# Experts of a three-layer network: PSUM tiles dealt out anew, and the second group's rows located earlier

## The chip, the cores and the metric

The kernel runs on one core of one Trainium2 chip. The metric is the device time of one execution in microseconds (us). Three executions of the kernel before took 1882.86, 1884.65 and 1886.02 us; the median, 1884.65 us, is the time that a prediction is set against.

## The reference, cut to what matters

The network has three layers over 512 tokens of width 1024: two of mixers and dense feed-forward blocks, and one of attention followed by a mixture of experts. The change lies in that mixture alone, the last part of the program:

```python
def _hierarchical_moe(xt, w_rg, b_rg, w_re, b_re, w_gate, w_up, w_down):
    ...
    expert_id = g_idx * EXPERTS_PER_GROUP + top_i
    combine = jnp.sum(jax.nn.one_hot(expert_id, N_EXPERTS, dtype=jnp.float32)
                      * (g1 * g2)[..., None], axis=1).astype(xt.dtype)
    y = jnp.zeros_like(xt)
    for e in range(N_EXPERTS):
        he = jax.nn.silu(xt @ w_gate[e]) * (xt @ w_up[e])
        y = y + combine[:, e:e + 1] * (he @ w_down[e])
    return y
```

There are 32 experts; every token goes to two of them. Each expert has a gate and an up matrix of 1024 x 256 and a down matrix of 256 x 1024, 3 MB of float32 in all. After the sum the tokens are normalized once more and written out.

## The kernel before, in words

Routing (`tail`, L1506) gives every token two experts and a slot among the 64 rows that each expert has room for. The normalized tokens lie in DRAM (`hd`). The function `moe` (L1626) then works on **pairs** of experts (two times 64 rows fill the 128 partitions; 16 pairs, numbered p) and on **groups** of two pairs (8 groups, numbered g). Its steps are small functions:

- `locate(g)` (L1632) finds which token sits in which of the group's 256 slots. Four `pick`s on VectorE (L1486 to L1488, one for each 128 tokens) write the one-hot matrix `s1`; group 0's were made during routing. Eight place products on TensorE (L1641, six columns each, four for each pair) give each slot's token number and gate weight in a PSUM tile; VectorE makes an index (`ix`, L1644), ScalarE copies two columns (`wsl`, L1650), VectorE adds them (`ws`, L1653), and GpSimd starts an indirect gather (L1646) of the pair's 128 rows from `hd` into `xg`, of which there are three buffers.
- `spread(g)` (L1657) transposes `s1` on TensorE (L1662, two PSUM tiles) and ScalarE copies it (`ST`, L1665). `s1` is one buffer: the next group's picks write it after these transposes.
- `turn(p, j)` (L1668) transposes one half of the gathered rows (L1675, four transposes into one PSUM tile), copied to `mhT` by VectorE (j = 0, L1680) or ScalarE (j = 1, L1678).
- `gate_up(p)` (L1682) is 16 matmuls in one PSUM tile (L1688), then SiLU on ScalarE (`msi`, L1691) and the product on VectorE (`mhe`, L1694).
- `inner(p)` (L1698) transposes `mhe` (L1701, one PSUM tile); ScalarE copies it (`heT`, L1703).
- `down(p)` (L1706) is eight matmuls in two PSUM tiles (L1711), taken out by ScalarE (L1716) and VectorE (L1717).
- `combine(g)` (L1721) adds a group's results to the tokens: 32 matmuls in eight PSUM tiles (L1729), each added by VectorE (L1732).

TensorE's order is written out by hand (`manual_schedule`): what stands first in the program runs first there. The order of the other engines is planned by the framework, which also chooses which of a tag's buffers a tile gets. PSUM has eight banks, and every tile here takes one. They are dealt out by tags: `psum(mm=4, tp=2, px=2)` at L1529 gives four to matrix products (`mm`), two to transposes and place products (`tp`) and two to the combination (`px`). A new tile of a tag waits until the readers of the tile that it replaces are done.

The loop's order for each pair p is: `turn(p + 2, 0)`, `inner(p)`, `turn(p + 2, 1)`, `down(p)`, `gate_up(p + 1)`, and then `locate(p // 2 + 2)` after an even p, or `combine(p // 2)` and `spread(p // 2 + 2)` after an odd one.

SyncE's queue issues the weights: the gate and up matrices of a pair (4 MB, `unit`, L1610) go into rings that hold three pairs, the down matrices (2 MB, `load_down`, L1603) into a ring of two. A pair's next load is issued once the matmuls that read the buffer are done: `load_up(3)` behind `gate_up(0)`, `load_down(p + 2)` behind `down(p)`, `load_up(p + 4)` behind `gate_up(p + 1)`. Three pairs of the one and two of the other are loaded ahead, during routing.

Of the kernel before, what the change touches and what calls it, by code (L numbers as in the profile page):

```python
# [91 lines left out]
class Builder:  # L92
# [1533 lines left out]
    def moe(self, st, s1, weights, downs):  # L1626
        nc = self.nc
        mp = self.pool("moe")
        NG, NPAIR = NE // 4, NE // 2
        grp, rows, hTs = {}, {}, {}  # L1630

        def locate(g):  # L1632

            if g:
                for tt in range(NT):
                    self.pick(g, tt, st, s1)
            ws = []
            for i in range(2):
                pw = self.ps("tp")
                for tt in range(NT):  # L1640
                    nc.tensor.matmul(pw[:, 0:6], s1[:, tt, i * P:(i + 1) * P], st["cw"][:, tt, 2 * g + i, :],  # L1641
                                     start=tt == 0, stop=tt == NT - 1)
                ix = self.t(mp, "ix", [P, 1], U32, bufs=4)
                nc.vector.tensor_scalar(ix, pw[:, 4:5], float(T), None, op0=ALU.add)  # L1644
                xg = self.t(mp, "xg", [P, D], bufs=3)
                nc.gpsimd.indirect_dma_start(xg, None, self.hd[:, :], bass.IndirectOffsetOnAxis(ap=ix, axis=0))  # L1646
                rows[2 * g + i] = xg
                w = self.t(mp, "ws", [P, 1], bufs=6)
                wl = self.t(mp, "wsl", [P, 2], bufs=2)
                nc.scalar.activation(wl, pw[:, 2:4], AF.Copy)  # L1650
                for j in range(2):
                    r = slice(64 * j, 64 * j + 64)
                    nc.vector.tensor_tensor(w[r], pw[r, j:j + 1], wl[r, j:j + 1], op=ALU.add)  # L1653
                ws.append(w)
            grp[g] = [ws]

        def spread(g):  # L1657

            for i in range(2):
                p = self.ps("tp")  # L1660
                for tt in range(NT):
                    nc.tensor.transpose(p[:, tt * P:(tt + 1) * P], s1[:, tt, i * P:(i + 1) * P].bitcast(F32),  # L1662
                                        self.ident)
                s = self.t(mp, "ST", [P, T], F32R, bufs=4)
                nc.scalar.activation(s, p, AF.Copy)  # L1665
                grp[g].append(s)

        def turn(p, j):  # L1668

            xg = rows[p]  # L1670
            if j == 0:
                hTs[p] = self.t(mp, "mhT", [P, KD, P], bufs=2)
            tp = self.ps("tp")
            for i in range(4):
                nc.tensor.transpose(tp[:, i * P:(i + 1) * P], xg[:, (4 * j + i) * P:(4 * j + i + 1) * P], self.ident)  # L1675
            pv = tp.rearrange("p (a b) -> p a b", a=4)
            if j:
                nc.scalar.activation(hTs[p][:, 4:8, :], pv, AF.Copy)  # L1678
            else:
                nc.vector.tensor_copy(hTs[p][:, 0:4, :], pv)  # L1680

        def gate_up(p, u):  # L1682
            ws, hT = grp[p // 2][0], hTs[p]
            ps = self.ps()
            for kb in range(KD):
                for e in range(2):
                    r = slice(64 * e, 64 * e + 64)
                    nc.tensor.matmul(ps[r, :].rearrange("p (j n) -> p j n", j=2), hT[:, kb, r], u[kb // 4][e][:, :, kb % 4, :],  # L1688
                                     start=kb == 0, stop=kb == KD - 1)
            s = self.t(mp, "msi", [P, 256])  # L1690
            nc.scalar.activation(s, ps[:, 0:256], AF.Silu)  # L1691
            he = self.t(mp, "mhe", [P, 256], bufs=2)
            v = lambda z: z.rearrange("t (p k) -> t p k", k=2)
            nc.vector.scalar_tensor_tensor(he.rearrange("t (k p) -> t p k", k=2), v(s), ws[p % 2], v(ps[:, 256:512]),  # L1694
                                           op0=ALU.mult, op1=ALU.mult)
            return he

        def inner(p, he):  # L1698
            tp = self.ps("tp")
            for f in range(2):  # L1700
                nc.tensor.transpose(tp[:, f * P:(f + 1) * P], he[:, f * P:(f + 1) * P], self.ident)  # L1701
            heT = self.t(mp, "heT", [P, 256], bufs=2)
            nc.scalar.activation(heT, tp[:, 0:256], AF.Copy)  # L1703
            return heT

        def down(p, heT, rv):  # L1706
            dn = [self.ps() for _ in range(2)]
            for hf in range(2):
                for f in range(2):
                    for e in range(2):  # L1710
                        nc.tensor.matmul(dn[hf][64 * e:64 * e + 64, :], heT[:, f * P + 64 * e:f * P + 64 * e + 64],  # L1711
                                         rv[e][:, f, hf * 512:(hf + 1) * 512], start=f == 0, stop=f == 1)
            ye = []
            for hf in range(2):
                yh, yl = (z[p % 2 * 2 + hf] for z in self.yroom)
                nc.scalar.activation(yh, dn[hf], AF.Copy)  # L1716
                nc.vector.tensor_tensor(yl, dn[hf], yh.bitcast(F32), op=ALU.subtract)  # L1717
                ye.append((yh, yl))
            return ye

        def combine(g, ye, then=None):  # L1721
            ST = grp[g][1:]
            for tt in range(NT):
                for hf in range(2):
                    p = self.ps("px")
                    n = 0
                    for i in range(2):
                        for z in ye[i][hf]:
                            nc.tensor.matmul(p, ST[i][:, tt * P:(tt + 1) * P], z, start=n == 0, stop=n == 3)  # L1729
                            n += 1  # L1730
                    xs = self.x[:, tt, hf * 512:(hf + 1) * 512]
                    nc.vector.tensor_tensor(xs, p, xs, op=ALU.add)  # L1732
                if then and tt:
                    then(tt - 1)
            if then:
                then(NT - 1)

        with self.tc.manual_schedule(engines={mybir.EngineType.PE}):
            locate(0)
            spread(0)  # L1740
            for j in range(2):
                turn(0, j)
            he = gate_up(0, weights[0])
            weights.append(self.load_up(3))
            for j in range(2):
                turn(1, j)
            locate(1)
            spread(1)
            ye, last = [], None
            for p in range(NPAIR):  # L1750
                if p + 2 < NPAIR:
                    turn(p + 2, 0)
                heT = inner(p, he)
                if p + 2 < NPAIR:
                    turn(p + 2, 1)
                ye.append(down(p, heT, downs[p]))
                if p + 2 < NPAIR:
                    downs.append(self.load_down(p + 2))
                if p + 1 < NPAIR:
                    he = gate_up(p + 1, weights[p + 1])  # L1760
                    if p + 4 < NPAIR:
                        weights.append(self.load_up(p + 4))
                else:
                    last = self.final()
                if p % 2 == 0 and p // 2 + 2 < NG:
                    locate(p // 2 + 2)
                if p % 2:
                    combine(p // 2, ye, last)
                    ye = []
                    if p // 2 + 2 < NG:  # L1770
                        spread(p // 2 + 2)
        self.done(mp)
# [248 lines left out]
```

## Time and profile before

| | us |
|---|---|
| median of three runs | 1884.65 |
| the profiled execution, its own time | 1883.5 |
| its span, first to last instruction | 1881.8 |
| TensorE busy over the span | 1786.6 (95%) |
| VectorE busy | 922.6 (49%) |
| ScalarE busy | 626.5 (33%) |
| GpSimd busy | 164.6 (9%) |

All times in the profile are counted from the span's start. TensorE is busy nearly throughout, but a matmul's record includes pipeline time, and its clock may be at half speed, so the share alone does not say what a stage is worth. The experts begin near 1554 us and the last result is written at the end of the span. The mean granted TensorE clock over the span is 0.971 of full speed.

### The profile page before, as it was taken

The numbers are of one execution on the slowest core, as the hardware profiler recorded it, in microseconds if no ns is written. First come the engines' busy times: TensorE is split into PE (matmuls) and PEld (weight loads), VectorE is DVE, ScalarE is ACT, GpSimd is POOL, SyncE is SP. The second block draws the span as 40 slices with busy tenths as digits, with TensorE's granted clock in tenths as the row PEclk, the third lists the DMA queues.
The fourth block names the chain that finished last, engine by engine and source line by source line (L and its number), as shares of the span: only waits on it lengthen the run. The fifth ranks groups of instructions, "written<-read, shape, count | busy, mean of one in ns | idle before, by whom it ended". The sixth has DMA issues, their size and how long they took to land. (4 is left out here: it accounts for less than half of the span.)

```text
span 1881.8 us, 23441 instructions
## 1 busy us (share of the span) xinstructions
PE 1786.6 (95%) x9314; PEld 1367.1 (73%) x9315; DVE 922.6 (49%) x1637; ACT 626.5 (33%) x1152; POOL 164.6 (9%) x312
## 2 busy tenths in 40 slices
PE   8999999999999999999999999998999976999997
PEld 6788888888799876778888888876876763444443
DVE  7654444444645345555444444465455563334334
ACT  6333222222431334554322222245556421111112
POOL 1001000000232110002000000020000121000000
PEclk9999999999999996999999999999999986999999
DMA  6433223222331301043232232242312294999972
GB/s 231 148 134 132 93 90 105 97 90 90 111 125 56 90 25 44 1 144 103 90 112 90 90 111 90 68 140 87 92 46 83 80 339 176 374 369 376 348 305 86
DMA packets 136308, 257.01 MB, mean 137 GB/s; under 512 B 11319, under 2 KB 88023, under 8 KB 131971
## 3 DMA queue, kind: packets, MB, share of 16 engines
q1 hardware_dynamic: 124000, 231.89, 35.5%
q10 hardware_dynamic: 9282, 13.10, 2.1%
q0 software_dynamic: 2912, 10.49, 1.4%
q8 instruction: 75, 1.23, 0.3%
q14 instruction: 39, 0.31, 0.0%
HBM read 247.04 MB, written 11.03 MB: 137 GB/s over the span
## 5 line engine op out<-in xcount | busy, mean ns | idle before, releaser
L173 PE MATMUL mm<-acth,whi 128*128 128x512 f32 (+2 forms) x968 | 368.9, 381 | 0.0
L174 PE MATMUL mm<-actl,whi 128*128 128x512 f32 (+2 forms) x968 | 365.0, 377 | 0.0
L175 PE MATMUL mm<-acth,wlo 128*128 128x512 f32 (+2 forms) x968 | 364.4, 376 | 0.0
L150 DVE TENSOR_TENSOR wlo<-raw,whi 128x2048 fp32r<-128x2048 f32 (+1 forms) x96 | 218.7, 2279 | 247.6 <-ACT whi L149 247.4
L149 ACT ACTIVATE whi<-raw 128x2048 fp32r<-128x2048 f32 (+1 forms) x96 | 182.5, 1901 | 435.0 <-issue 195.2
L173 PEld LDWEIGHTS mm<-acth,whi 128*128 128x128 f32 (+1 forms) x968 | 182.0, 188 | 35.2 <-issue 2.4
L175 PEld LDWEIGHTS mm<-acth,wlo 128*128 128x128 f32 (+1 forms) x968 | 182.0, 188 | 34.5 <-issue 0.2
L174 PEld LDWEIGHTS mm<-actl,whi 128*128 128x128 f32 (+1 forms) x968 | 182.2, 188 | 33.6 <-issue 1.0
L173 PE MATMUL mm<-whi,acth 128*128 128x256 f32 (+2 forms) x480 | 160.2, 335 | 2.1 <-ACT gate L707 1.7
L174 PE MATMUL mm<-wlo,acth 128*128 128x256 f32 (+2 forms) x480 | 158.1, 330 | 0.6 <-DVE wlo L150 0.6
L175 PE MATMUL mm<-whi,actl 128*128 128x256 f32 (+2 forms) x448 | 145.6, 327 | 0.4 <-DVE actl L204 0.3
L173 PE MATMUL px<-whi,hidh 128*128 128x512 f32 x352 | 137.4, 390 | 0.6 <-DVE macc L331 0.6
L175 PE MATMUL px<-whi,hidl 128*128 128x512 f32 x352 | 137.9, 392 | 0.0
L174 PE MATMUL px<-wlo,hidh 128*128 128x512 f32 x352 | 137.4, 390 | 0.0
L331 DVE TENSOR_TENSOR macc<-px,macc 128x512 f32<-128x512 f32 x144 | 97.6, 688 | 75.3 <-PE px L175 75.3
L173 PEld LDWEIGHTS mm<-whi,acth 128*128 128x128 f32 x480 | 91.4, 191 | 10.2 <-ACT gate L707 1.9
L174 PEld LDWEIGHTS mm<-wlo,acth 128*128 128x128 f32 x480 | 91.2, 190 | 8.4 <-DVE wlo L150 1.3
L175 PEld LDWEIGHTS mm<-whi,actl 128*128 128x128 f32 x448 | 85.1, 190 | 7.2 <-DVE actl L204 1.0
L173 PEld LDWEIGHTS px<-whi,hidh 128*128 128x128 f32 x352 | 66.1, 188 | 16.4 <-DVE macc L331 1.5
L311 DVE TENSOR_TENSOR hidf<-mm,silu 128x512 f32<-128x512 f32 x44 | 30.4, 690 | 94.8 <-PE mm L175 94.8
L175 PEld LDWEIGHTS px<-whi,hidl 128*128 128x128 f32 x352 | 66.1, 188 | 14.1 <-DVE hidl L313 0.5
L174 PEld LDWEIGHTS px<-wlo,hidh 128*128 128x128 f32 x352 | 66.1, 188 | 13.2
(427 smaller groups left out, 2683.8 us busy)
## 6 DMA issues: line engine op xcount, KB each, us to landing
raw<-in_ffn_w_gate SPq DMA_DIRECT2D x22, 1024.0 KB, 5.2
raw<-in_ffn_w_up SPq DMA_DIRECT2D x22, 1024.0 KB, 5.3
raw<-in_ffn_w_down SPq DMA_DIRECT2D x22, 1024.0 KB, 4.8
mixd<-in_w_expert_down SPq DMA_DIRECT2D x16, 1024.0 KB, 6.9
down<-in_w_expert_down SPq DMA_DIRECT2D x16, 1024.0 KB, 9.1
raw<-in_od_w_in SPq DMA_DIRECT2D x12, 1024.0 KB, 5.0
raw<-in_w_expert_gate SPq DMA_DIRECT2D x18, 512.0 KB, 8.4
raw<-in_w_expert_up SPq DMA_DIRECT2D x18, 512.0 KB, 8.3
```

The source lines that it names most:

```text
L149: self.nc.scalar.activation(hi[:, :n], raw[:, :n], AF.Copy)
L150: self.nc.vector.tensor_tensor(lo[:, :n], raw[:, :n], hi[:, :n].bitcast(F32), op=ALU.subtract)
L173: mm(out, l[0], r[0], start=first, stop=False)
L174: mm(out, l[0], r[1], start=False, stop=False)
L175: mm(out, l[1], r[0], start=False, stop=last)
L311: nc.vector.tensor_tensor(hf, pu[f], s, op=ALU.mult)
L331: nc.vector.tensor_tensor(m, p, m, op=ALU.add)
```

## The change

The PSUM pool is released and opened anew at the head of `moe`, with three tiles for matrix products, three for transposes and two for the combination. The place products of `locate` take their tiles from the combination's tag. And `locate(1)` moves from behind the second pair's transposes to the place between `spread(0)` and the first pair's.

```diff
@@ -1627,6 +1627,7 @@
         nc = self.nc
         mp = self.pool("moe")
         NG, NPAIR = NE // 4, NE // 2
+        self.psum(mm=3, tp=3, px=2)
         grp, rows, hTs = {}, {}, {}
 
         def locate(g):
@@ -1636,7 +1637,7 @@
                     self.pick(g, tt, st, s1)
             ws = []
             for i in range(2):
-                pw = self.ps("tp")
+                pw = self.ps("px")
                 for tt in range(NT):
                     nc.tensor.matmul(pw[:, 0:6], s1[:, tt, i * P:(i + 1) * P], st["cw"][:, tt, 2 * g + i, :],
                                      start=tt == 0, stop=tt == NT - 1)
@@ -1738,13 +1739,13 @@
         with self.tc.manual_schedule(engines={mybir.EngineType.PE}):
             locate(0)
             spread(0)
+            locate(1)
             for j in range(2):
                 turn(0, j)
             he = gate_up(0, weights[0])
             weights.append(self.load_up(3))
             for j in range(2):
                 turn(1, j)
-            locate(1)
             spread(1)
             ye, last = [], None
             for p in range(NPAIR):
```

## Rows read from the trace of the kernel before

**Rows 1.** The page's 40 slices of the span: DMA busy share, in tenths.

```profile
DMA  6433223222331301043232232242312294999972
```

**Rows 2.** TensorE's waits, 1605 to 1830 us: total us, times, longest.

```profile
PE tp L1675 <- ACT heT L1703: 5.7, 12, 0.5
PE tp L1675 <- ACT wsl L1650: 5.3, 5, 1.1
```

**Rows 3.** Windows: PE, PEld, DVE, ACT, POOL busy, PEclk, DMA share, GB/s.

```profile
1580.00:1584.00 4.00, 0.00 (x0) 0.00 (x0) 1.78 (x6) 0.00 (x0) 0.00 (x0) 0.50 1.02 415
1588.00:1592.00 4.00, 4.00 (x12) 1.56 (x14) 0.51 (x3) 0.60 (x1) 0.00 (x0) 0.50 0.01 5
1668.28:1705.86 37.58, 35.32 (x166) 16.71 (x164) 15.00 (x34) 6.55 (x14) 1.88 (x2) 0.95 0.96 363
```

**Rows 4.** Timeline of the experts' opening: start, us, engine, line, [idle before <- releaser].

```profile
1558.59 1.23 PE L1641 MATMUL tp<-cw,s 128*128 128x6 f32 x5 [2.43 <-POOL cw L1459]
...
1559.44 1.11 POOL L1646 DMA_INDIRECT xg<-hd,ix  x1 [0.91 <-DVE ix L1644]
...
1564.34 1.94 PE L1675 MATMUL tp<-ident,xg 128*128 128x128 f32 x8 [2.01 <-DMA xg<-hd,ix]
...
1564.66 0.48 DVE L1488 SCALAR_TENSOR_TENSOR s<-iota,sl,sa 128x256 fp32r<-128x256 f32 x1
...
1574.62 1.09 PE L1675 MATMUL tp<-ident,xg 128*128 128x128 f32 x8
...
1577.20 0.94 POOL L1646 DMA_INDIRECT xg<-hd,ix  x1 [15.38 <-DVE ix L1644]
...
1585.87 1.08 PE L1675 MATMUL tp<-ident,xg 128*128 128x128 f32 x4 [6.61 <-DMA xg<-hd,ix]
...
1588.90 5.61 PE L1711 MATMUL mm<-mixd,heT 128*64 128x512 f32 x16
```

**Rows 5.** Timeline of two passages from place products to a down projection.

```profile
1601.30 1.05 PE L1641 MATMUL tp<-cw,s 128*128 128x6 f32 x8
...
1605.33 3.65 PE L1711 MATMUL mm<-down,heT 128*64 128x512 f32 x16
...
1637.42 1.05 PE L1641 MATMUL tp<-cw,s 128*128 128x6 f32 x8
...
1638.59 0.65 DVE L1694 SCALAR_TENSOR_TENSOR mhe<-msi,ws,mm 128x256 f32<-128x256 f32 x1
...
1639.54 0.63 PE L1675 MATMUL tp<-ident,xg 128*128 128x128 f32 x4 [1.06 <-ACT wsl L1650]
1640.00 0.38 PE L1701 MATMUL tp<-ident,mhe 128*128 128x128 f32 x2
...
1640.42 0.38 ACT L1703 ACTIVATE heT<-tp 128x256 f32<-128x256 f32 x1 [1.54 <-PE tp L1701]
...
1641.90 4.71 PE L1711 MATMUL mm<-down,heT 128*64 128x512 f32 x16
```

**Rows 6.** Timeline of one passage from spread to a down projection.

```profile
1623.70 1.03 PE L1662 MATMUL tp<-ident,s 128*128 128x128 f32 x8
...
1624.33 1.09 ACT L1665 ACTIVATE ST<-tp 128x512 fp32r<-128x512 f32 x2 [8.03 <-PE tp L1662]
...
1624.98 0.66 PE L1675 MATMUL tp<-ident,xg 128*128 128x128 f32 x4 [0.25 <-ACT ST L1665]
...
1626.97 3.65 PE L1711 MATMUL mm<-mixd,heT 128*64 128x512 f32 x16
```

**Rows 7.** DMA issue to landing, down loads (L1607), then gate and up loads (L1618).

```profile
DMA to landing us min/median/max: 4.7/6.9/15.1
...
DMA to landing us min/median/max: 5.0/10.7/14.5
```

**Rows 8.** Timeline behind the down projection of 1605.33: next weights, last evacuation.

```profile
1608.38 0.14 PEld L1688 LDWEIGHTS mm<-whi,mhT 128*64 128x64 f32 x1 [0.28 <-issue]
...
1609.68 0.69 DVE L1717 TENSOR_TENSOR acth<-mm,acth 128x512 fp32r<-128x512 f32 x1 [1.05 <-ACT acth L1716]
```

## The prediction

> **What bounds the kernel now.** I read four views, from the whole to the single instruction. First the page's slices: the last seven of the forty carry the experts, and DMA, at 4 tenths in the first of them, stands at 9 in the four that follow, so it could be the limit [rows 1]. TensorE's waits settle that: from 1605 to 1830 us that view lists four lines, the two largest are shown, and none names a DMA; it waits for ScalarE and VectorE to empty transpose tiles [rows 2]. So TensorE's order sets the pace and the weight buffers follow. The windows give the tempo: from the end of one even pair's down projection to the next is 37.58 us (two pairs, one group), and the four such stretches after 1630 agree within 0.1 us; DMA is busy 0.96 of one [rows 3]. Last the timeline. At the opening TensorE transposes pair 0's rows at 1564.34, works until pair 1's transposes at 1574.62, starts group 1's gather only at 1577.20, and then stands for 6.61 us until those rows land; the down projection behind it starts at 1588.90 and takes 5.61 us where others take 3.65 [rows 4, 5]. Meanwhile DMA runs dry as well: from 1588 to 1592 its share is 0.01 [rows 3]. In the loop there are two kinds of passage between the big products: from the place products to a down projection (six times, groups 2 to 7), 4.03 us at 1601.30 and 4.48 us the five times after it, and from spread to a down projection (six times), 3.27 us [rows 5, 6]. The five longer ones hold a fall of the clock to its lower level: their down projections take 4.71 us or nearly, against 3.65 [rows 5].
>
> **The change part by part.** *The earlier locate(1).* What it issues moves with it: four picks, two indices and four adds on VectorE, two small copies on ScalarE, eight place products, two gathers on GpSimd. It passes pair 0's transposes and first products and pair 1's transposes. On VectorE the picks cost nothing new: they were already made early, the last one from 1564.66 to 1565.14 [rows 4]. On TensorE the place products now stand ahead of pair 0's transposes and must wait for that last pick. Five remain then, at 1.23/5 = 0.25 us each at the lower clock [rows 4], so the transposes start near 1565.14 + 0.06 + 1.23 = 1566.4 instead of 1564.34: **2.1 us later**. Queued behind them are gate_up(0) and, on SyncE's queue, load_up(3), which issues 2.1 us later too; DMA ran dry later in the opening, so that costs nothing by itself. I take no credit for a clock that might rise sooner.
>
> On GpSimd nothing else is queued. The gather for pair 2 starts near 1565.8; the first one took from 1559.44 to 1564.34, 4.9 us, on idle DMA, so it lands near 1570.7. The fourth gather needs one of three row buffers and waits for pair 0's transposes, until about 1568.4; pair 3 is needed a pair later. With pair 1's transposes now near 1574.62 + 2.1 = 1576.7, the rows of pair 2 have been there for 6 us, and the wait of 6.61 us goes. From there to the first down projection lie pair 1's transposes (1.09 us) and one spread passage at its new length, 3.27 - 1.0 = 2.3 us (below): 1580.1. At the upper clock it takes 3.65 us and ends at 1583.75; before it ended at 1588.90 + 5.61 = 1594.51. **Gain 10.8 us**. If TensorE still waits between those steps, or the clock is low once more (5.61 - 3.65 = 2.0 us), it is 8 to 9; if the clock rises sooner, 11.5.
>
> *Place products in the combination's tiles.* Now the transposes behind them wait 1.06 us for the readers of the place products' tile [rows 5]. That wait goes; late next is mhe, which inner needs: it ends at 1638.59 + 0.65 = 1639.24. From inner's first transpose to heT is 0.42 us, heT takes 0.38 [rows 5], and with a third tile the second half's transposes run under that copy. So the down projection starts at 1639.24 + 0.1 + 0.42 + 0.38 + 0.06 = 1640.2, that is 2.8 us after the place products. The passage shortens by 4.03 - 2.8 = 1.2 us once and by 4.48 - 2.8 = 1.7 us five times: **9.7 us**. Nearest bounds: were mhe ahead of the indices on VectorE, 0.45 us more for each; were the second half still to wait for heT, 0.6 us less for each: 6.1 to 12.4. The combination's tiles are free then: its last product lies a pair back and its next lies behind a down projection and a gate_up, over 10 us on; if the two met, its first tile would wait some 2 us once a group.
>
> *A third transpose tile.* In the spread passage the first transposes wait 0.25 us, the second half waits about 0.47 more for heT [rows 2, 6]. With three tiles ScalarE's order is the limit: its two copies end at 1624.33 + 1.09 = 1625.42, heT ends 0.38 us and a hand-over later at 1625.85, and the down projection starts at 1625.95 instead of 1626.97: 1.0 us, six times: **6.0 us**; if the second half still waits, half of that.
>
> *The clock's falls.* Five of the six place passages cost 4.71 - 3.65 = 1.06 us in the down projection behind them; what they cost in the passage is counted above. The spread passages, which hold about 0.7 us of idle in 3.27, show none in six [rows 6]; the new place passage holds about 0.6 us of idle in 2.8 and is nearest to that. I take the falls as gone: **5.3 us**, between 0 and 5.3. *TensorE: Matmul & The Clock Gate* of the Trainium skill, in its section on psum-queue depth-cycling, tells of micro-idles between groups of matmuls, as PSUM tiles are cycled, that make the clock swing; fewer product tiles would speak against this change there. By it the falls stay, and the sum is 5.3 us less, which is the first rival.
>
> *One product tile fewer.* A pair uses three: two for down, one for gate_up. With three, gate_up(p + 1) gets the tile that gate_up(p) left, last read by mhe before inner starts, and down(p + 1) gets those of down(p), a gate_up earlier. Cost nothing; the cover is that order. If it got down's second tile it would wait from 1608.38 to 1610.37, 2.0 us for each pair [rows 8]. *Releasing the pool* makes the first tiles wait for routing's last readers; the first place products wait 2.43 us for the gate weights anyway [rows 4].
>
> *DMA behind a faster TensorE.* A group would take 37.58 - 1.7 - 1.0 - 1.06 = 33.8 us, while DMA was busy 0.96 x 37.58 = 36 us of one: the backlog grows by about 2 us a group, 10 us over five. A down load is issued at the end of down(p) and needed at down(p + 2), about 33 us later and after the change 29; it lands within 15.1 us [rows 7]. That leaves 14 us; I give 5 of them to a start without the dry stretch and 10 to the backlog, so it just runs out in the last groups: I charge **2 us**, between 0 and 7.
>
> **Sum:** 10.8 + 9.7 + 6.0 + 5.3 - 2 = 29.8 us. The span of 1881.8 us becomes 1852.0, and the profiled execution's 1883.5 becomes 1853.7. The median of the runs shown is 1.15 above that execution; I forecast 1884.65 - 29.8 = **1854.8 us**. Its own range, from the bounds that are likely together, is 1848 to 1859.
>
> **The rivals.** *The clock still falls.* The passages at 1601 and 1637 are alike up to the down projection, yet one shows a fall and the other doesn't, so a shorter passage may still have one [rows 5]. Then 5.3 us are not gained, and with less haste DMA keeps up: 31.8 - 5.3 = 26.5, 1858.2 us. *DMA becomes the bound from the start of the loop.* A group then takes 36 us: 10.8 + 6 x 1.6 = 20.4 us, 1864.2 us. For it: a share of 0.96 and a ring of only two down loads. Against it: no DMA wait now, and loads that land half a group early. *DMA: Bandwidth & Descriptors* of the Trainium skill, section Specifications, gives a limit of about 358 GB/s of memory bandwidth for a core; by it the loop, at 363 GB/s, could not be quicker, the gain would be the opening's 10.8 us alone, and the time 1873.9. The trace disagrees with it: 415 GB/s from 1580 to 1584 [rows 3]. *The early gather gives nothing* (the picks fall behind other work on VectorE): 31.8 - 10.8 - 2.1 = 18.9 us, 1865.8 us. *The third tile is not used as meant*: the framework, not the text, gives each tile its buffer, and if the transposes wait as now, the opening's 10.8 us are left: 1873.9 us.
>
> *Slower: gate_up waits for down's evacuation.* If the framework gives it down's second tile, each of 15 pairs waits 2.0 us [rows 8], 30 us, and a stop in front of the longest product costs the clock as well: 1.06 us in the ten pairs that show no fall now, 10.6 us. Against these stand 31.8 - 5.3 = 26.5 us. 1884.65 + 30 + 10.6 - 26.5 = 1898.8 us. It decides above a wait of 26.5/15 = 1.8 us a pair, or about 1.1 with the clock. Against it: a tile that is long free exists each time.
>
> **How the numbers follow.** Forecast 0.58; clock 0.12; DMA 0.12 (0.02 of it the stricter limit); early gather 0.05; third tile 0.05; slower rival 0.08, of which 0.03 ends within 0.2% of the time before, about what a measurement can tell from no change. So faster by more than that 0.92, within it 0.03, slower 0.05. The range 1847 to 1866 takes in the forecast with its bounds (a little of it lies outside), the clock, most of the DMA case and the early gather: about 0.82.
>
> **What would show it.** Right: no wait of TensorE for a gather before the first down projection, which starts near 1580 and takes 3.65 us; place passages of 2.8 us, spread passages of 2.3; no half-speed stretch in the loop; a group of about 34 us with DMA above 0.98 and, in the last groups, first waits for weights. Wrong: a wait of L1688 for L1717, a down projection that waits for its load in every pair, transposes that still wait for heT, or a first gather for group 1 that still starts behind gate_up(0).

## The result, and the profile after

Four executions of the changed kernel took 1849.75 to 1855.62 us, the median is **1854.75 us**; beside them the kernel before took 1882.86 to 1886.02, median 1884.39. The ratio is 0.9826, with a 95% interval of 0.9808 to 0.9845. The forecast was 1854.8, in a range of 1847 to 1866. The profiled execution took 1854.36 us, its span is 1852.6 (before: 1881.8), so 29.2 us of span are to be found. After line 1630 the changed kernel's lines stand one lower.

The page's DMA slices, after:

```profile
DMA  7433322232232211023323322223311256999982
```

The last seven slices, 4, 9, 9, 9, 9, 7, 2 before [rows 1], now read 6, 9, 9, 9, 9, 8, 2. A slice lasts some 46 us here and is not the same stretch of the program as before, so the dry stretch is better read from windows. One of the kernel after (columns as in [rows 3]):

```profile
1588.00:1592.00 4.00, 4.00 (x22) 1.29 (x18) 0.00 (x0) 0.00 (x0) 0.00 (x0) 1.00 1.01 410
```

From 1576 us on, no such window of 4 us in the opening has a DMA share under 0.92; before, the share was 0.01 just behind the start of the first down projection [rows 3].

TensorE's waits from 1605 to 1830 us are two lines (the answer to [rows 2], which add up to 11.0 us in their two largest lines alone):

```profile
PE tp L1702 <- DVE mhe L1695: 3.3, 7, 1.2
PE mm L1712 <- ACT heT L1704: 0.5, 1, 0.5
```

The waits for heT and for wsl are gone; late next is mhe, as the prediction had it, and no DMA is named.

The opening on the timeline (the answer to [rows 4]; start, us, engine, line, and in brackets the idle time before and what ended it):

```profile
1560.35 1.22 PE L1642 MATMUL px<-cw,s 128*128 128x6 f32 x5 [2.44 <-POOL cw L1459]
...
1565.75 0.48 DVE L1488 SCALAR_TENSOR_TENSOR s<-iota,sl,sa 128x256 fp32r<-128x256 f32 x1
...
1566.29 1.23 PE L1642 MATMUL px<-cw,s 128*128 128x6 f32 x5 [0.60 <-DVE s L1488]
...
1567.13 0.94 POOL L1647 DMA_INDIRECT xg<-hd,ix  x1 [3.54 <-DVE ix L1645]
...
1567.38 1.97 PE L1676 MATMUL tp<-ident,xg 128*128 128x128 f32 x8
...
1578.07 1.09 PE L1676 MATMUL tp<-ident,xg 128*128 128x128 f32 x8
...
1580.07 0.60 PE L1676 MATMUL tp<-ident,xg 128*128 128x128 f32 x4
...
1581.14 0.41 PE L1702 MATMUL tp<-ident,mhe 128*128 128x128 f32 x2 [0.48 <-DVE mhe L1695]
```

Pair 2's gather starts at 1567.13 instead of 1577.20, and its transposes at 1580.07 wait for no transfer; the 6.61 us are gone. The first down projection starts at 1582.03 and takes 3.65 us. One thing in these rows is not the change's: the first row, the last place products of group 0, starts 1.76 us later than before, though nothing ahead of it was edited. Nearly the same difference, 1.74 us, stands on both timelines already at a routing product (L1470, 1551.70 before and 1553.44 after) ahead of the experts. So times are counted from that row here, up to the end of the last down projection, and called the **section**: before 1558.59 to 1863.16, 304.57 us; after 1560.35 to 1833.92, 273.57 us. The section is 31.0 us shorter; less the 1.76 us, that is the span's 29.2.

One place passage and one spread passage of the kernel after, to be set beside [rows 5, 6]:

```profile
1613.63 1.04 PE L1663 MATMUL tp<-ident,s 128*128 128x128 f32 x8
...
1614.26 1.09 ACT L1666 ACTIVATE ST<-tp 128x512 fp32r<-128x512 f32 x2 [8.02 <-PE tp L1663]
...
1615.39 0.38 ACT L1704 ACTIVATE heT<-tp 128x256 f32<-128x256 f32 x1
1615.40 0.42 PEld L1676 LDWEIGHTS tp<-ident,xg 128*128 128x128 f32 x4 [0.29 <-ACT ST L1666]
...
1615.99 3.65 PE L1712 MATMUL mm<-mixd,heT 128*64 128x512 f32 x16
...
1626.44 1.05 PE L1642 MATMUL px<-cw,s 128*128 128x6 f32 x8
...
1627.61 0.65 DVE L1695 SCALAR_TENSOR_TENSOR mhe<-msi,ws,mm 128x256 f32<-128x256 f32 x1
...
1628.31 0.44 PE L1702 MATMUL tp<-ident,mhe 128*128 128x128 f32 x2 [0.30 <-DVE mhe L1695]
1628.59 0.60 PE L1676 MATMUL tp<-ident,xg 128*128 128x128 f32 x4
...
1629.22 3.65 PE L1712 MATMUL mm<-down,heT 128*64 128x512 f32 x16
```

Spread: 1613.63 to 1615.99, 2.36 us. Place: 1626.44 to 1629.22, 2.78 us. All six of each are within 0.02 us of these, and every down projection takes 3.65 us. Windows of two groups, from down projection to down projection (columns as in [rows 3]):

```profile
1615.99:1649.96 33.97, 33.59 (x165) 16.15 (x164) 14.99 (x35) 6.56 (x14) 1.88 (x2) 1.00 1.02 412
1649.96:1683.93 33.97, 33.58 (x166) 16.16 (x165) 15.00 (x35) 6.56 (x14) 1.88 (x2) 1.00 1.02 396
```

DMA issue to landing, of the down loads and then of the gate and up loads, where [rows 7] had medians of 6.9 and 10.7:

```profile
DMA to landing us min/median/max: 6.8/7.1/14.4
...
DMA to landing us min/median/max: 4.8/12.6/14.5
```

A group takes 33.97 us where it took 37.58 [rows 3], at the clock's upper level throughout, and DMA moves 396 to 412 GB/s where it moved 363.

Of all executions reported below one is left out: a sixth one of the last kernel in the table took 4420.90 us, while the other five took 1845.41 to 1852.91.

### The profile page after: what moved, and what is told of

The parts are those of the page before. It is cut to its first block, busy times and chain, and to the rows that moved or that the text cites. A ratio compares the mean times of both kernels' runs of the same rounds, so it can differ in the third digit from the quotient of the medians.

```text
span 1852.6 us, 23444 instructions
## 1 busy us (share of the span) xinstructions
PE 1777.0 (96%) x9314; PEld 1365.1 (74%) x9315; DVE 923.3 (50%) x1637; ACT 627.4 (34%) x1152; POOL 163.1 (9%) x312
```

## The experiments

Twelve further kernels were timed, and each has one profile. Since the place where the section begins moved between 1558.40 and 1567.33 us among them (one, told below, aside) with the same instructions ahead of it, the section is the measure that tells a few us apart; the times are given beside it. The section itself moves by about 1 us with gate_up(0), on whose way the clock rises: it took 8.8 us in the profile of the kernel after, 7.7 to 7.8 in those of seven later kernels, and 9.4 in one.

| kernel | time, median us (runs) | ratio to before on the same chip, 95% | section, us |
|---|---|---|---|
| before | 1884.39 (4) | | 304.57 |
| after | 1854.75 (4) | 0.9826 [0.9808, 0.9845] | 273.57 |
| early locate only | 1877.83 (7) | 0.9949 [0.9929, 0.9968] | 297.73 |
| both tile edits, old order | 1863.04 (4) | 0.9870 [0.9843, 0.9898] | 282.29 |
| place products in px only | 1879.07 (9) | 0.9950 [0.9932, 0.9969] | 296.62 |
| third transpose tile only | 1861.86 (4) | 0.9862 [0.9838, 0.9886] | 283.45 |
| after, no down loads | 1853.77 (4) | 0.9830 [0.9801, 0.9859] | 272.57 |
| after, two product tiles | 1857.23 (4) | 0.9837 [0.9809, 0.9866] | 272.58 |
| after, turn(0) ahead of locate(1) | 1854.40 (5) | 0.9832 [0.9809, 0.9855] | 274.29 |
| after, extra copies in the loop | 1856.00 (4) | 0.9831 [0.9804, 0.9858] | 272.59 |
| after, mm 2, tp 3, px 3 | 1848.38 (5) | 0.9811 [0.9786, 0.9837] | 269.94 |
| after, mhe ahead of the indices | 1851.28 (4) | 0.9806 [0.9779, 0.9833] | 269.33 |
| the last two together | 1849.45 (5) | 0.9803 [0.9779, 0.9827] | 266.81 |

### The parts of the change, one at a time

**The early locate(1) alone** (the kernel after with the other two edits undone):

```diff
-        self.psum(mm=3, tp=3, px=2)
...
-                pw = self.ps("px")
+                pw = self.ps("tp")
```

> Only locate(1) is moved ahead of pair 0's transposes; PSUM tiles as before. Theory (each wait pays where it stands): the 6.61 us wait for pair 2's rows goes, the first down projection takes 3.65 us instead of 5.61, but the opening's transposes still wait for two tiles, so the opening gains 8 to 10.6 us; the loop keeps its place passages of 4.0 to 4.5 us, its spread passages of 3.27 us and its falls of the clock: 1874 to 1876.5 us. Rival (the earlier start is worth nothing without the tiles, since the loop's weights then come late): 1880 us or more, with TensorE waiting for weights.

It gained 6.8 us of section. Its opening did what it was to do: the first down projection starts at 1586.23, 23.95 us after the section's begin instead of 30.31, and takes 3.65 us instead of 5.61: 8.3 us. The loop gave 1.5 back: all six place passages now take 4.48 us and show the fall, where before the first took 4.03 without one (0.45 + 1.06). The time, 1877.83, lies 1.3 us above the expected range, and that loss, which was not expected, accounts for it.

**Both tile edits, the old order** (locate(1) back behind turn(1)):

> Only the PSUM tiles change (three for products, three for transposes, place products in the combination's); locate(1) stays behind pair 1's transposes. Theory: place passages 2.8 us, spread passages 2.35 us, no falls of the clock in the loop, so 9.7 + 5.5 + 5.3 = 20.5 us, and about 1 us in the opening where the 6.6 us wait stays: 1862.5 to 1865 us. Rival (falls of the clock have another cause than the idle time in the place passages): the passages shorten as much but falls stay, 1868 us or more.

It gained 22.3 us of section. Passages 2.78 and 2.36, no fall in the loop; the opening's first down projection at the lower level again, 4.71 us. 22.3 + 6.8 = 29.1; the 1.9 that are missing to 31.0 are the falls and the first passage that the early part alone had lost (1.5), and what the two share in the opening (8.3 and 1.9 apart, 10.6 together).

**The place products in px alone** (four product and two transpose tiles, old order):

> Only the place products move into the combination's tiles; two transpose tiles, four product tiles, old order. Theory: the first transposes no longer wait 1.06 us, but the second half still waits for heT, so place passages take about 3.4 us, spread passages stay at 3.27: 6 us from the passages; falls of the clock go or stay (this run tells which), 0 to 5.3 us: 1873 to 1878 us. Rival (the third tile carries everything, this part nothing): 1883 us or more.

It gained 8.0 us of section; the time came out 1 us above what was expected, within the scatter of where the section begins. The passage shrinks to 3.37 us (one takes 3.71, since the clock falls within it), and two of six down projections still show the fall. TensorE's rows ahead of one that does, of this kernel:

```profile
1713.10 1.05 PE L1641 MATMUL px<-cw,s 128*128 128x6 f32 x8
1714.01 0.66 PE L1675 MATMUL tp<-ident,xg 128*128 128x128 f32 x4
1714.97 0.44 PE L1701 MATMUL tp<-ident,mhe 128*128 128x128 f32 x2 [0.30 <-DVE mhe L1694]
1715.88 0.66 PE L1675 MATMUL tp<-ident,xg 128*128 128x128 f32 x4 [0.47 <-ACT heT L1703]
1716.47 5.35 PE L1711 MATMUL mm<-down,heT 128*64 128x512 f32 x16
```

The windows of that passage and of the first 1.5 us of its down projection:

```profile
1713.10:1716.50 3.40, 2.62 (x22) 1.98 (x20) 2.05 (x8) 1.11 (x4) 1.87 (x2) 1.00 1.04 296
1716.50:1718.00 1.50, 1.50 (x5) 0.50 (x6) 0.00 (x0) 0.60 (x1) 0.00 (x0) 0.50 0.90 243
```

The clock is at 1.00 in the passage and at 0.50, the lower of its two levels (1.2 GHz), behind it. The passage at 1640.56 of the same kernel has the same rows with the same two waits and no fall: its down projection takes 3.65. So with these waits it goes either way. (The same holds in the kernel before: its first passage at 4.03 us and the five at 4.48 have the same waits of 1.06 and 0.47 us, and the 0.45 us between them is what the lower clock costs within the passage.)

**The third transpose tile alone** (place products still in tp, old order):

> Only the third transpose tile (and one product tile fewer); place products stay in transpose tiles, old order. Theory: the first transposes take the free third tile, inner waits for the place products' readers about as long as for mhe, so place passages take about 3.0 us and spread passages 2.35: 8.5 + 5.5 us, and the falls of the clock go with the idle time, 5.3 us: 1864 to 1867 us, within 2 us of both tile parts together. Rival (the two tile parts pay separately, 9.7 us for the place products' tile alone): 1873 us or more.

It gained 21.1 us of section, more than expected: this one edit alone brings two thirds of the whole. Of these, 8.0 come from the place passages, 5.5 from the spread passages, 5.3 from the falls, and 2.4 from the opening, which the expectation had left out. The spread passage is at 2.36, and the place passage falls to 3.08, though its place products still sit in the transposes' tiles. TensorE's rows:

```profile
1633.68 1.05 PE L1642 MATMUL tp<-cw,s 128*128 128x6 f32 x8
1634.60 0.66 PE L1676 MATMUL tp<-ident,xg 128*128 128x128 f32 x4
1635.84 0.41 PE L1702 MATMUL tp<-ident,mhe 128*128 128x128 f32 x2 [0.59 <-DVE ws L1654]
1636.20 0.63 PE L1676 MATMUL tp<-ident,xg 128*128 128x128 f32 x4
1636.76 0.65 PE L1712 MATMUL mm<-down,heT 128*64 128x512 f32 x2
```

With three tiles the first transposes find a free one; it is inner that waits for a place product's readers (ws), 0.59 us, and not 1.06 [rows 5]. None of the six falls. Behind this the move to px is worth 0.30 us a passage, 1.8 in all, of which the section shows 1.2, as this kernel's opening was 0.5 us shorter.

### What the transfers allow

**No down loads in the loop:**

```diff
-        for e in range(2):
+        for e in range(2 if p < 2 else 0):
```

> The changed kernel without the down matrices' loads of pairs 2 to 15 (28 MB less; those pairs use the matrices of pairs 0 and 1, so the output is not the reference's). DMA then has a third less to move in the loop. Theory (TensorE alone sets the pace, DMA at a share of 1.01 just keeps up): nothing moves, group 34.0 us, 1852 to 1857 us. Rival (DMA is the bound in the loop, or slows it by queueing): the group falls below 33.5 us and the time to 1850 us or less.

The passages are the same to 0.01 us, a group takes 33.97, at 276 to 282 GB/s from the second group on (350 in the first). TensorE alone sets the pace of the kernel after. (The section is 1.0 us shorter than after's, which is gate_up(0): 7.8 us here, 8.8 there.)

**Extra copies, first try:** a copy of 1 MB from memory to memory for each pair, written behind load_down.

> The changed kernel with one more transfer of 1 MB for each pair behind its down load, copied from an expert's matrix to unused DRAM (nothing reads it): 15.7 MB a group instead of 13.6. Theory (DMA is at its limit near 405 GB/s): a group wants 38.8 us, 4.8 more than now, less the lead of the rings (up to 10 us over the loop): 1870 to 1885 us, and TensorE waits for weights. Rival (there is room, the share overstates): below 1860 us.

This run says nothing on the question. Time 1882.11 (10 runs), ratio 0.9978 [0.9959, 0.9996], but its section takes 272.50 us. The copies' row, with issue times:

```profile
L1761 SPq DMA_DIRECT2D spare<-in_w_expert_down x14: 488/587/11236, 3.5 to 68.2; - x14
```

Nothing tied them to the loop, and the planner issued all fourteen in the program's first 68 us, ahead of the loads that the first layer waits for; the experts began 26 us late, and the loop never saw a copy.

**Extra copies, tied to the loop,** half a megabyte each:

```diff
+            last = self.nc.sync.dma_start(rv[e], ...)
+        if p >= 2:
+            spare = self.dr.tile([128, D], F32, ...)
+            with self.tc.issue_after(last.ins):
+                self.nc.sync.dma_start(spare, self.A["w_expert_down_2"][0][2 * p][0:128, :])
```

> The kernel after, plus a copy of 0.5 MB from memory to memory for each pair from the third on, put on SyncE's queue behind that pair's down weights (tied to the load ahead of it, so that it stays in the loop; the copies' result is used by nothing). A group then reads 14.7 MB and writes 1.0 MB in place of reading 13.6 MB. Theory (the transfers had room in the kernel after, TensorE sets the pace, but the room is small): at the 400 to 412 GB/s that the groups showed, 14.7 MB want 35.7 to 36.7 us and TensorE gets through a group in 33.97, so the group grows by 1.7 to 2.7 us, six times: 10 to 16 us, 1865 to 1871, with TensorE waits for a DMA in the rows. Rival (412 GB/s is only what TensorE let through, and the queue can do far more): groups stay within 0.3 us of 33.97, no TensorE wait for a DMA, 1853 to 1857. If the write counts like a read, 15.7 MB: 38 to 39 us a group, 1879 to 1886.

The groups did not grow: 272.59 us of section, no TensorE wait for a transfer, as the rival said. Its reason is another matter. Windows of two groups of this kernel:

```profile
1687.97:1721.94 33.97, 33.58 (x165) 16.15 (x164) 15.00 (x35) 6.55 (x14) 1.87 (x2) 1.00 1.02 413
1721.94:1755.91 33.97, 33.58 (x166) 16.16 (x165) 14.97 (x34) 6.54 (x14) 1.88 (x2) 1.00 1.02 414
```

Its queue's waits for TensorE from 1590 to 1800 us (in total, times, longest):

```profile
SPq L1607 <- PE mm L1716: 8.6, 3, 5.5
...
SPq L1622 <- PE mm L1693: 3.3, 3, 1.9
```

The same of the kernel after:

```profile
SPq L1607 <- PE mm L1712: 42.7, 12, 5.1
...
SPq L1618 <- PE mm L1689: 25.1, 13, 2.6
SPq L1618 <- PE px L1642: 11.5, 6, 1.9
```

After, the queue stood 79 us of these 210 waiting for TensorE to free a buffer (42.7 + 25.1 + 11.5). With the copies the two largest such waits come to 12 (all to 17), the rate stays at 397 to 414 GB/s (a copy counted once), and the queue falls behind: the last weight load was issued 2.4 us ahead of a down projection in the kernel after (1783.43 to 1785.83), and 10.0 us behind the same one here (1799.91 to 1789.88). Twelve us of lead were eaten in seven groups and never ran out. So both halves of the question have an answer: with the queue behind, the rate went no higher than 414 GB/s, and the loads' lead covers at least 12 us.

### The rivals on tiles and order

**Two product tiles** (same order of instructions on every engine):

```diff
-        self.psum(mm=3, tp=3, px=2)
+        self.psum(mm=2, tp=3, px=2)
```

> The changed kernel with two product tiles instead of three (one bank unused), the same order of instructions. Theory: gate_up then takes the tile of down's first half and waits some 0.3 us for VectorE to empty it, 15 times, 4 to 5 us, no falls: 1857 to 1861 us. Rival (as the prediction's slower rival priced it: a wait of 2.0 us in each pair and the clock falls with it): 1880 us or more.

Even one tile fewer costs nothing: section 272.58, groups 33.96. The wait that the slower rival spoke of does appear then, in PE's weight loads of this kernel:

```profile
PEld mm L1689 <- DVE acth L1718: 8.8, 15, 0.6
```

Fifteen times 0.6 us, and no group is longer: the weight load waits while the down projection's products still run. In the kernel after this row does not exist. The time, 1857.23, lies in the expected range, but not for the expected reason: no group grew, and in the profiled execution, 1858.84, the section began at 1566.35, 6 us later than in the kernel after.

**turn(0) ahead of locate(1):**

> The changed kernel with locate(1) behind pair 0's transposes and still ahead of gate_up(0). Theory (the place products' wait for the last pick delays pair 0's transposes by 1.3 to 2.1 us): the transposes start as in the kernel before, the place products run while VectorE copies mhT, the gather for pair 2 starts 1 us later and is still on time: 1 to 1.5 us faster than the changed kernel, 1852.5 to 1854 us. Rival (gather too late): slower, up to 1860 us, with a wait of TensorE for the gathered rows.

Nothing gained. Pair 0's transposes start 5.71 us into the section (after: 7.03), having waited 2.65 us for their own gather. The place products now lie between them and gate_up(0), which starts at 9.10 (after: 8.92) and takes 9.36 us (after: 8.80); the first down projection starts at 22.42, not before 21.68. The place products that the change put ahead of turn(0) fill time in which those rows were on their way.

### What was late next

**Three tiles for the combination** (two for products):

```diff
-        self.psum(mm=3, tp=3, px=2)
+        self.psum(mm=2, tp=3, px=3)
```

> The kernel after with the eight PSUM banks divided as two product tiles, three transpose tiles and three combination tiles, the same instructions in the same order. Theory: the run with two product tiles showed that the third one does nothing; the combination of a group, 32 products of 0.2135 us, takes about 7.9 us instead of 6.8 because each tile's addition on VectorE (0.69 us) and its two hand-overs do not fit behind one tile's four products (0.85 us); with three tiles TensorE is a tile further ahead, and 0.8 to 1.1 us a group go, in seven or eight groups: 1846 to 1849, if the transfers keep up (13.6 MB in 33 us are 412 GB/s). Rival: the combination waits for something else, or the transfers bind at 404 GB/s; 1852 to 1856, and then TensorE shows waits for a DMA.

A combination takes 7.72 us instead of 8.08, a group 33.60, 0.37 less; the expected 0.8 to 1.1 was too much. The waits did go: the kernel after has 46 of PE's weight loads waiting 12.1 us for the combination's additions, here (1590 to 1840 us) there are two. The row of the kernel after, then of this one:

```profile
PEld px L1730 <- DVE actl L1733: 12.1, 46, 1.3
...
PEld px L1730 <- DVE actl L1733: 1.2, 2, 0.7
```

What is left is TensorE's own pace: the additions on VectorE now start 0.93 us apart and each waits 0.24 us for its four products, 0.234 us a product. I had taken 0.2135, from gate_up's. The time, 1848.38, still lies in the expected range; in the profiled execution, 1848.06, that goes with the section's early begin, 1558.40, and not with the gain.

**mhe ahead of the indices on VectorE:**

```diff
+                with self.tc.issue_after(self.he_ins.ins) if g > 1 else contextlib.nullcontext():
+                    nc.vector.tensor_scalar(ix, pw[:, 4:5], float(T), None, op0=ALU.add)
...
+            self.he_ins = nc.vector.scalar_tensor_tensor(he.rearrange("t (k p) -> t p k", k=2), ...)
```

> The kernel after with VectorE's instructions in the place passages in another order: the gated product of the pair goes ahead of the two index additions of the group being located (the third group on), which stood ahead of it and waited for the place products. Theory: TensorE's wait of 0.3 us for the gated product ahead of the inner transposes goes, the place passage falls from 2.78 to about 2.45 us, six times 0.3: 1.8 us, 1852 to 1854, hardly to be told from 1854.75 by the time; the passages tell it. Rival: the passage is set by the transposed rows' evacuations, and stays at 2.78; or the gathers, then 0.2 us later, cost something.

The place passage takes 2.26 us, 0.52 less, more than the wait of 0.30 that I counted:

```profile
1628.33 1.05 PE L1642 MATMUL px<-cw,s 128*128 128x6 f32 x8
...
1628.89 0.67 DVE L1696 SCALAR_TENSOR_TENSOR mhe<-msi,ws,mm 128x256 f32<-128x256 f32 x1 [5.96 <-ACT msi L1693]
...
1629.74 0.38 PE L1703 MATMUL tp<-ident,mhe 128*128 128x128 f32 x2
...
1630.59 1.94 PE L1713 MATMUL mm<-down,heT 128*64 128x512 f32 x8
```

inner now runs straight behind the first transposes, so that no pause stands between the two; the prediction had put 0.45 us on this order, as a bound. The section is 3.3 us below that of the kernel with the extra copies, whose gate_up(0) took nearly as long (7.80 us there, 7.76 here).

**Both edits.**

> The two edits together: two product tiles, three transpose tiles, three combination tiles, and the gated product ahead of the index additions. Theory: the gains add, 8 to 10 us: 1844 to 1848. Rival: the transfers, at 404 to 412 GB/s with the engines' share at 1.0 or over, take back what is gained beyond some 33.0 to 33.7 us a group: 1848 to 1853 with TensorE waits for a DMA at the gate and up products or the down products.

A group takes 33.09 us, at 397 GB/s in the first and 411 to 413 in the five behind it:

```profile
1646.44:1679.53 33.09, 33.01 (x166) 16.59 (x165) 14.83 (x35) 6.44 (x14) 1.87 (x2) 1.00 1.02 412
```

The gains add: 5.8 us of section (272.59 - 266.81), no TensorE wait for a transfer. This is the shortest section of all, 6.8 us below that of the kernel after, 1.1 of it gate_up(0)'s. The median time, 1849.45, lies 1.5 us above the expected range and 1 us above that of the three combination tiles alone. So by time this version is faster than the kernel before; that it is faster than the kernel after the times do not show, since the intervals of the two ratios overlap (0.9779 to 0.9827 and 0.9808 to 0.9845), and only the section does.

## Why the prediction was right, step by step

**The opening, 10.8 us.** From the section's begin to the end of the first down projection: 35.92 us before, 25.33 after, **10.6**. Inside, small errors cancel. Pair 0's transposes moved by 1.28 us and not 2.1, since the spread transposes no longer wait for the place products' readers and the picks come 0.7 us sooner; gate_up(0) took 8.8 instead of 8.4; and from pair 1's transposes to the first down projection it is 3.96 us (1578.07 to 1582.03) and not 3.4, as inner waits 0.48 us for mhe there.

**Place passages, 9.7 us.** 4.03 + 5 x 4.48 - 6 x 2.78 = **9.75**. Late next was mhe, and the half that follows ran under heT's copy, as worked out. The text gave the gain to the px move, with the third tile as a condition; the runs with one edit each show that either brings most of the 1.70 us by itself (3.08 us with the third tile alone, 1.40 less than 4.48; 3.37 with px alone, 1.11 less), so it cannot be given to one of them. The sum did not depend on the split.

**Spread passages, 6.0 us.** 6 x (3.27 - 2.36) = **5.5**. The passage is 0.1 us longer than worked out: the step took heT as the limit, but the second half's transposes need a tile that ST's second copy leaves at 1614.26 + 1.09 = 1615.35, start at 1615.40 and end behind heT.

**The clock's falls, 5.3 us.** **5.3**: no down projection of the loop is above 3.65. Here lay a choice between 0 and 5.3 that no row decided; the runs now bound it: with 1.53 us of waits in the place passage eleven falls in twelve (five in six before, six in six with the early locate alone), with 0.77 us two in six, with 0.59 and with 0.30 none in six each. With the 0.45 us that each fall cost in the passage, which the prediction counted there, the falls were worth 7.6 us in all. The windows of the kernel after show 1.00 in all groups. *TensorE: Matmul & The Clock Gate* of the Trainium skill, in its section on psum-queue depth-cycling, had spoken for a clock that still swings, which was the first rival, 1858.2; the trace does not bear it out here.

**One product tile fewer, nothing.** Nothing: no row of the kernel after waits for a product tile's readers, and in the run with two tiles the next one fewer cost nothing either.

**DMA behind a faster TensorE, 2 us.** This step failed: measured **0**. It took a share of 0.96 in a group of 37.58 us as 36 us of work that does not shrink, and so a backlog of 2 us a group. The same weights went through in 33.97 us, at 396 to 412 GB/s, and the first waits for weights that the prediction named as a sign never came. The share was 0.96 at 363 GB/s and 1.01 to 1.02 at 396 to 412, so it does not say how much more could go. The rate was there to be seen in the opening, 415 GB/s [rows 3], and 13.6 MB (363 GB/s x 37.58 us) at that rate want 32.9 us, below TensorE's 33.8. I used that row only against the rival of the stricter limit, and not in my own sum. (For that rival *DMA: Bandwidth & Descriptors* of the Trainium skill, section Specifications, had given the 358 GB/s, which six groups at 396 GB/s and more contradict as well. The same page of the Trainium skill, section Bandwidth, gives 425 GB/s for a load of 16 MB by a core whose neighbour is idle, and sets the 358 down to two busy cores; the groups at 396 to 414 lie under that figure.)

**Sum.** 10.6 + 9.75 + 5.5 + 5.3 = 31.1, against a section of 31.0. Less the 1.76 us by which the part ahead ran later in this execution, 29.3. The parts of the change were right in mechanism and, but for DMA, in size. That the median meets the forecast to 0.05 us is luck: the 2 us too much for DMA stand against 1.76 us that belong to no part of the change, and the four executions lie 5.9 us apart.

**The rivals.** The clock still falls: no, by all groups at 1.00. DMA as the bound: no, by the run without down loads; at 13.6 MB and 414 GB/s it would, by estimate, begin near 33 us a group, and the last kernel runs at 33.09 without a wait. The early gather gives nothing, the third tile is not used: no, by the opening's and the passages' rows. Slower by gate_up's wait: the wait exists only with two product tiles, and costs nothing there.

## What to carry to other kernels

A DMA share near 1 is no demand: divide the bytes of a period by the best rate that the same trace shows, and compare that with the time that the engines need. Where several small steps pass through a pool of PSUM tiles, count the tiles in flight in each passage between long products: one more there, alone, brought 21 us of section where the whole change brought 31, and a tile that another tag did not need paid for it. Parts that shorten the same passage overlap: the three alone add up to 35.9 us (6.8 + 8.0 + 21.1). Count differences of a few us from a row just ahead of the change, since what lies before it moves by more than that from one execution to the next.

## What the runs showed of the hardware that was not expected

Place passages with 0.77 us of waits, 3.37 us long, let TensorE's clock fall to its lower level in two of six; with 0.59 us of waits, 3.08 us long, it never fell in six, and with 1.53 us it fell in eleven of twelve. The waits alone do not decide it: spread passages with 0.72 us of waits in 3.27 us never showed a fall, in eighteen of them (six each before, with the early locate alone and with px alone). What a wait costs is then more than its length: 0.45 us more in the passage and 1.06 in the down projection behind it before, and 1.3 and 1.7 us in the two down projections with px alone. And one core's loads went on at 411 to 413 GB/s for five groups of 33.1 us on end, with a share of 1.02, where a share of 0.96 before stood beside 363.
